# The low-part matmul of an attention score block over 128 array rows instead of 64

## The chip, the cores and the metric

The kernel runs on one core of a Trainium2 chip. The metric is the device time of one launch in microseconds (us), the median of several executions. All work is in 32-bit floats; the matmuls take operands of the type fp32r, and the kernel keeps the accuracy by splitting an operand into a high and a low part and adding up the products.

## What is computed

Two layers of a decoder block on 512 tokens of width 1024. Each layer projects the normalised tokens once; the columns go to a state-space mixer (SSD), a stick-breaking attention of four heads and a block-sparse softmax attention with ALiBi (MoBA) of four heads, all heads 64 wide. Then come an output projection and a SwiGLU FFN.

```
def hybrid_layer(x, ...):
    h = rms_norm(x, pre_mix_norm)
    proj = h @ w_in
    z, xbc, dt_raw, sb_qkv, moba_qkv = jnp.split(proj, [o1, o2, o3, o4], axis=-1)
    y_ssd = ssd_mixer(z, xbc, dt_raw, ...)
    ...
    y_sb = _merge_heads(stick_breaking_attention(q, k, v))
    ...
    y_moba = _merge_heads(moba_attention(q, k, v, alibi_slopes(MOBA_HEADS)))
    ...
    mix = jnp.concatenate([y_ssd, y_sb, y_moba], axis=-1) @ w_out
    x = x + rms_norm(mix, post_mix_norm)
    h2 = rms_norm(x, pre_ffn_norm)
    f = (jax.nn.silu(h2 @ w_gate) * (h2 @ w_up)) @ w_down
    return x + rms_norm(f, post_ffn_norm)

def stick_breaking_attention(q, k, v):
    ...
        z = jnp.einsum('bhqd,bhkd->bhqk', q[:, :, start:end], k[:, :, :end]) * scale
        ...
        log_keep = jnp.where(strict, jax.nn.log_sigmoid(-z), 0.0)
        after = lax.cumsum(log_keep, axis=3, reverse=True) - log_keep
        w = jnp.where(strict, jnp.exp(jax.nn.log_sigmoid(z) + after), 0.0)
```

The change touches the score products of both attentions: `z` here, and the logits of MoBA, which are a product of the same kind over the 64 columns of a head.

## The kernel before

**Staging.** Everything of a layer stays on the chip: 128-partition tiles of 512 columns, named `F0` to `F44`, `R0` to `R7` and `x00` to `x31` (the residual stream), and eight PSUM banks `B0` to `B7`. The weights stream in chunks of 512 KB (`chunk`): SyncE issues the load into `wr`, ScalarE makes the high part `wh` (L108), VectorE the low part `wl` (L109). A projection (`fm_mm`, matmul at L210; `tok_proj`, L201) makes three passes for each of eight 128-row slices of the contraction.

**The score products.** `qk_pair` makes, for two heads, five tiles. `tiles[2 + h]` is the stationary operand of head h: the high part in the head's own 64 partitions (`own`, 0 to 63 for h = 0, 64 to 127 for h = 1) and the low part in the other 64. `tiles[h]` is the moving operand with the high part in both halves, so that one matmul over 128 rows (L300) gives high times high plus low times high. `tiles[4]` holds the low parts of the moving operand of both heads, each in its own 64 partitions. The second matmul (L301) adds high times low: it runs over the head's 64 rows alone, `tiles[2 + h][rows, cs]` against `tiles[4][rows, cd]`.

**Loops.** In stick-breaking attention (`sb_head`, heads 0 to 3), key block i of 3, 2, 1, 0 makes a score block of 128, 256, 384 and 512 columns: the pair L300 and L301, a mask matmul (L315, bf16), then softplus on VectorE and ScalarE (L220, L143, L223), the split of its result (L108, L109), the cumulative sum as matmuls (L322), exp, and the product with v (L329). In MoBA, query block j of 0 to 3 and head h make the pair with 128 to 512 columns, then L425, exp, transposes (L431) and the product with v (L435). So there are 4 heads times 4 blocks in each attention, 32 pairs in a layer and 64 in all, 16 of each width.

**Order.** A scheduler fixes each engine's order when the kernel is built. It mixes the matmuls of the attentions with those of projections that are ready (L210: q and k of the next heads, x, B and C of the SSD; the dt projection L349, and L356, which adds up its parts with 16 rows), so that TensorE has work while VectorE and ScalarE make the softplus.

**GpSimd** has little to do: the power -1/2 of the norms (L155, 50 instructions of one to four columns), and from its queue the DMAs of the decay rows (L379, L387).

**Tiles that are shared.** The twenty q/k tiles of a layer take the places `F4` to `F11` and `x00` to `x31` (`QNAMES`) in groups of five. The last pair of MoBA takes the first group's tiles again. Afterwards the places serve other things: `load_x` fetches the residual again (L99), and `F4` to `F11` hold z and the mixer's output. `XBC`, the SSD's inputs, is `F12` to `F19`.

Of the kernel before, what the change touches and what calls it, by code (L numbers as in the profile page):

```python
# [8 lines left out]
F32 = mybir.dt.float32  # L9
# [7 lines left out]
P = 128  # L17
D = 1024
S = 512
NT = S // P  # L20
# [37 lines left out]
def trunk(ctx, tc, x, wch, wdt, gains, mixgain, conv, small, ident_d, consts_d, stack_d, out):  # L58
# [6 lines left out]

    F = [None if 4 <= i < 12 else cp.tile([P, 512], F32, name=f"F{i}") for i in range(NF)]
    R = [cp.tile([P, 512], F32R, name=f"R{i}") for i in range(8)]
# [90 lines left out]
    def to_fm(srcs, dst, bank):  # L158
        """Token-major [128, 128] slices to feature-major hi and lo parts; dst(i, n) names n consecutive targets."""
        for q in range(0, len(srcs), 4):  # L160
            n = min(4, len(srcs) - q)
            p = bank()
            for i in range(n):
                T.transpose(p[:, i * P:(i + 1) * P], srcs[q + i], ident)  # L164
            dst(q, n, p)
# [27 lines left out]
    def tok_proj(l, c0, bank, evict, w=None):  # L193
        """512 columns, token-major: chunks c0..c0+3 each hold two k tiles."""
        w = w or [chunk(l, c0 + i) for i in range(4)]
        for t in range(NT):
            p = bank()
            n = 0
            for k in range(KT):
                for a, b in PASSES:  # L200
                    T.matmul(p, hT[a][:, k, t * P:(t + 1) * P], w[k // 2][b][:, (k % 2) * 512:(k % 2 + 1) * 512],  # L201
                             start=n == 0, stop=n == 3 * KT - 1)
                    n += 1
            evict(t, p)
# [19 lines left out]

    VT, XBC, LM = F[0:4], F[12:20], F[20:28]
    MIXA, MG = F[28:32], F[32:34]
    QNAMES = [f"F{i}" for i in range(4, 12)] + [f"x{t}{h}" for t in range(NT) for h in range(2)]
    take_jk = ring([F[0:2], F[2:4], F[43:45]])
# [31 lines left out]
    for l in range(DEPTH):  # L260
        # ---- input projection: v, q and k of both attentions, dt
        tok_proj(l, C_V, ring([B[0], B[2], B[4], B[6]]), lambda t, p: A.activation(VT[t], p, AF.Copy),
# [16 lines left out]
        def qk_pair(dup, stk, scale_dup, scale_stk, tiles):  # L279
            """Two heads: [hi; lo] of the stationary operand and [hi; hi] of the moving one, with the latter's lo."""  # L280
            low = tiles[4]
            p = fm_proj(l, dup, acc())
            with tc.high_priority(offset=EV_OFF):
                for h in range(2):
                    own, other, d = slice(h * 64, h * 64 + 64), slice(64 - h * 64, 128 - h * 64), tiles[h]
                    A.activation(d[own], p[own], AF.Copy, scale=scale_dup)
                    V.scalar_tensor_tensor(low[own], p[own], scale_dup, d.bitcast(F32)[own], op0=OP.mult, op1=OP.subtract)
                    A.activation(d[other], p[own], AF.Copy, scale=scale_dup)  # L288
# [9 lines left out]
        def qk_mm(p, tiles, h, cs, cd, stop):  # L298
            rows = slice(h * 64, h * 64 + 64)
            T.matmul(p, tiles[2 + h][:, cs], tiles[h][:, cd], start=True, stop=False, skip_group_check=True)  # L300
            T.matmul(p, tiles[2 + h][rows, cs], tiles[4][rows, cd], start=False, stop=stop, skip_group_check=True)  # L301

        # ---- stick-breaking attention, a head at a time
        sb_mx = ring(B[6:8])
# [29 lines left out]

        SB = [qk_pair(C_SQK, C_SQK + 2, 0.125, 1.0, QS[0:5])]
        exp_set()
        for h in (0, 1):
            if Q1POS == h + 1:
                SB.append(qk_pair(C_SQK + 1, C_SQK + 3, 0.125, 1.0, QS[5:10]))
            sb_head(h)  # L340
        if Q1POS == 0:
            SB.append(qk_pair(C_SQK + 1, C_SQK + 3, 0.125, 1.0, QS[5:10]))

# [50 lines left out]

        MB = [qk_pair(C_MQK + 2, C_MQK, 1.0, qs[:, 0:1], QS[10:15])]
        for h in (2, 3):
            if MBPOS == h - 1:
                MB.append(qk_pair(C_MQK + 3, C_MQK + 1, 1.0, qs[:, 1:2], QS[0:5]))
            sb_head(h)
        if MBPOS == 3:  # L400
            MB.append(qk_pair(C_MQK + 3, C_MQK + 1, 1.0, qs[:, 1:2], QS[0:5]))

# [8 lines left out]

        # ---- softmax attention with ALiBi
        mx = ring([B[3], B[4]])
# [34 lines left out]
        QF = [slot(f"F{i}") for i in range(4, 12)]  # L448
        ZS, MIX = QF[0:4], QF[4:8]
        xres[:] = [[slot(f"x{t}{h}") for h in range(2)] for t in range(NT)]  # L450
        for t in range(NT):
            load_x(t, x if l == 0 else xsave)

        # ---- x, B, C: projection, causal convolution, silu; z
        for i in range(8):
# [9 lines left out]

        # ---- SSD, chunk by chunk
        mx = ring(B[3:5])
# [68 lines left out]

        # ---- output projection, two token tiles at a time
        grow1 = load_row(gains[l, 1], F[41:43])
# [33 lines left out]

        # ---- FFN
        GT = F[12:20] + F[22:28] + QF
        take_p = ring([B[5:7], [B[7], B[0]], [B[2], B[4]], [B[1], B[3]]])
# [98 lines left out]
```

## Time and profile before

| what | value |
|---|---|
| median of 3 runs | 1283.4 us (1283.39 to 1283.61) |
| span of the profiled execution, first to last instruction | 1279.0 us |
| TensorE (PE) busy | 1254.5 us, 98% |
| TensorE weight loads (PEld) busy, beside the matmuls | 1040.3 us, 81% |
| VectorE (DVE) busy | 613.8 us, 48% |
| ScalarE (ACT) busy | 499.0 us, 39% |
| GpSimd (POOL) busy | 45.6 us, 4% |
| granted TensorE clock, mean | 0.999 of full speed |
| DMA | 128.70 MB, mean 101 GB/s |

The median lies 4.4 us above the span: what a launch takes outside the first and the last instruction. "Busy" of TensorE does not mean that the array works at its best: the ends of matmuls are modelled, and a matmul that stands behind something slow is shown as longer, not as a gap. So what a matmul costs in a row of them is read from the starts: the time from one start to the next, called a step here. A row of a timeline gives the start, the duration, the engine, the source line, what is written and read, the shape (rows*columns of the stationary operand, then rows x columns of the moving one) and how many instructions the row joins.

### The profile page before, as it was taken

To read this page: it belongs to the slowest core of one execution; us is meant where nothing else is said; L and a number is where in the kernel's file an instruction comes from. 1 tells how busy PE (TensorE), PEld (TensorE's weight loads), DVE (VectorE), ACT (ScalarE), POOL (GpSimd) and SP (SyncE) were. 2 spreads that over 40 slices of the span, in tenths; PEclk is the share of its full clock that TensorE was granted. 3 is DMA by queue.
4 is the path that set the end of the run, shared out by engine and by line. 5 is a ranking of instruction groups with operands and counts; after the bars stand their busy time and mean duration, and the time that the engine had idled before them with its cause. 6 is when DMAs were issued, how large, how long until landed. Compare 5 with 4: busy or idle time off the path is not lost.

```text
span 1279.0 us, 15353 instructions
## 1 busy us (share of the span) xinstructions
PE 1254.5 (98%) x6118; PEld 1040.3 (81%) x6118; DVE 613.8 (48%) x1011; ACT 499.0 (39%) x892; POOL 45.6 (4%) x72
## 2 busy tenths in 40 slices
PE   6999999999999999999999999999999999999997
PEld 5777788888888888888877788888988888888886
DVE  5456765884322222333465577478642222223334
ACT  5555655353222222322355556634432222222222
POOL 0010000010000000000000100001000000000000
PEclk9999999999999999999999999999999999999999
DMA  7331133333233332332333322222433333332321
GB/s 246 116 102 65 65 108 107 108 132 94 91 98 97 99 99 99 99 96 91 110 114 109 117 66 66 83 91 83 132 116 99 99 99 99 95 93 95 98 83 66
DMA packets 40760, 128.70 MB, mean 101 GB/s; under 512 B 5456, under 2 KB 5744, under 8 KB 40688
## 3 DMA queue, kind: packets, MB, share of 16 engines
q1 hardware_dynamic: 39344, 123.49, 30.3%
q0 software_dynamic: 1344, 4.23, 1.0%
q8 instruction: 48, 0.79, 0.3%
q14 instruction: 24, 0.20, 0.0%
HBM read 123.47 MB, written 4.23 MB: 100 GB/s over the span
## 4 chain that ended last, share of the span: by engine, by line
PE 95%; DVE 2%; ACT 1%; issue 1%; DMA 0%; SPq 0%; DVEq 0%; POOLq 0%; POOL 0%
PE B L210 51%; PE B L596 18%; PE B L201 7%; PE B L546 7%; PE B L301 2%; PE B L322 2%; PE B L329 1%; PE B L435 1%; PE B L300 1%; PE B L164 1%; PE B L506 1%; PE B L431 1%; PE B L349 1%; PE B L557 0%; PE B L512 0%
## 5 line engine op out<-in xcount | busy, mean ns | idle before, releaser
L210 PE MATMUL B<-hT,wh 128*128 128x512 f32 (+1 forms) x2048 | 609.1, 379 | 2.2 <-ACT F L288 2.2
L210 PEld LDWEIGHTS B<-hT,wh 128*128 128x128 f32 x2048 | 374.7, 188 | 73.4 <-ACT F L288 3.3
L210 PE MATMUL B<-hT,wl 128*128 128x512 f32 (+1 forms) x1024 | 386.6, 378 | 0.0
L109 DVE TENSOR_TENSOR wl<-wr,wh 128x1024 fp32r<-128x1024 f32 x204 | 248.6, 1224 | 254.7 <-ACT wh L108 253.2
L108 ACT ACTIVATE wh<-wr 128x1024 fp32r<-128x1024 f32 x204 | 214.9, 1057 | 392.8 <-PE B L210 314.5
L210 PEld LDWEIGHTS B<-hT,wl 128*128 128x128 f32 x1024 | 192.8, 188 | 34.5 <-issue 0.4
L596 PE MATMUL B<-wh,R 128*128 128x512 f32 x704 | 190.1, 389 | 0.0
L596 PEld LDWEIGHTS B<-wh,R 128*128 128x128 f32 x704 | 132.1, 188 | 27.3
L596 PE MATMUL B<-wl,R 128*128 128x512 f32 x352 | 110.0, 389 | 0.0
L109 DVE TENSOR_TENSOR R<-F,R 128x512 fp32r<-128x512 f32 (+2 forms) x76 | 45.9, 607 | 122.2 <-ACT R L108 121.9
L108 ACT ACTIVATE R<-F 128x512 fp32r<-128x512 f32 (+2 forms) x76 | 42.4, 560 | 143.6 <-PE B L596 139.0
L587 DVE TENSOR_TENSOR F<-B,F 128x512 f32<-128x512 f32 x44 | 30.4, 691 | 127.3 <-PE B L210 127.3
L201 PE MATMUL B<-wh,hT 128*128 128x512 f32 x256 | 83.2, 400 | 2.4 <-DVE hT L109 2.4
L596 PEld LDWEIGHTS B<-wl,R 128*128 128x128 f32 x352 | 66.1, 188 | 13.8
L546 PE MATMUL B<-wh,R 128*128 128x512 f32 x256 | 76.9, 398 | 0.0
L155 POOL TENSOR_TENSOR SM<-SM,mhalf 128x1 f32<-128x1 f32 (+2 forms) x50 | 35.5, 712 | 1097.7 <-DVE SM L154 793.7
L201 PEld LDWEIGHTS B<-wh,hT 128*128 128x128 f32 x256 | 48.1, 191 | 13.3 <-DVE hT L109 2.8
L546 PEld LDWEIGHTS B<-wh,R 128*128 128x128 f32 x256 | 47.6, 188 | 9.9 <-DVE R L109 0.4
L201 PE MATMUL B<-wl,hT 128*128 128x512 f32 x128 | 50.6, 396 | 0.0
L143 ACT ACTIVATE F<-F 128x512 f32<-128x512 f32 (+3 forms) x80 | 39.1, 498 | 21.0 <-DVE F L220 20.4
L546 PE MATMUL B<-wl,R 128*128 128x512 f32 x128 | 43.0, 394 | 0.0
L461 DVE SCALAR_TENSOR_TENSOR F<-B,cw,F 128x511 f32<-128x511 f32 (+2 forms) x48 | 35.8, 745 | 11.8 <-ACT F L459 11.2
(145 smaller groups left out, 988.2 us busy)
## 6 DMA issues: line engine op xcount, KB each, us to landing
wr<-in_wch_dram SPq DMA_DIRECT2D x204, 512.0 KB, 3.6
x<-in_x_dram SPq DMA_DIRECT2D x16, 256.0 KB, 3.2
F<-in_gains_dram SPq DMA_DIRECT2D x16, 256.0 KB, 4.3
F<-acd POOLq DMA_DIRECT2D x16, 256.0 KB, 6.4
xsave<-x SPq DMA_DIRECT2D x8, 256.0 KB, 2.0
x<-xsave SPq DMA_DIRECT2D x8, 256.0 KB, 2.9
out_dram<-x SPq DMA_DIRECT2D x8, 256.0 KB, 2.0
F<-in_mixgain_dram SPq DMA_DIRECT2D x4, 256.0 KB, 4.9
```

The costliest lines, as they stand in the source:

```text
L108: A.activation(hi, src, AF.Copy)
L109: return eng.tensor_tensor(lo, src, hi.bitcast(F32), op=OP.subtract)
L143: order["exp"][group] = A.activation(o, i, f, **kw)
L155: G.tensor_tensor(r, m, mhalf[:, 0:n], op=OP.pow)
L201: T.matmul(p, hT[a][:, k, t * P:(t + 1) * P], w[k // 2][b][:, (k % 2) * 512:(k % 2 + 1) * 512], start=n == 0, stop=n == 3 * KT - 1)
L210: T.matmul(p[:, t0 * P:t1 * P], w[b][:, k * P:(k + 1) * P], hT[a][:, k, t0 * P:t1 * P], start=first and n == 0, stop=n == 3 * KT - 1, skip ...
L301: T.matmul(p, tiles[2 + h][rows, cs], tiles[4][rows, cd], start=False, stop=stop, skip_group_check=True)
L322: T.matmul(pz[:, o:w], ntri if i2 == i else nones, s2, start=False, stop=i2 == NT - 1 and n == 1, skip_group_check=True)
L461: V.scalar_tensor_tensor(u[:, j:], p[:, :S - j], cw[:, i, 3 - j:4 - j], u[:, j:], op0=OP.mult, op1=OP.add)
L546: T.matmul(OB[j][hf], lt, w[b][:, hf * 512:(hf + 1) * 512], start=k == ks[0] and a == 0 and b == 0, stop=k == ks[-1] and a == 1)
L587: V.tensor_tensor(GT[i], pu, sg, op=OP.mult)
L596: T.matmul(B[2 * t + hf], gs[a][:, t * P:(t + 1) * P], w[b][:, hf * 512:(hf + 1) * 512], start=i == 0 and a == 0 and b == 0, stop=i == HT ...
```

## The change

`qk_pair` now makes six tiles: each head has a low tile of its own, `tiles[4 + h]`. GpSimd first fills the 64 partitions of the other head in it with zeros, VectorE writes the low part into the head's own 64 as before. The second matmul takes all 128 rows: the stationary operand is the same slice `tiles[2 + h][:, cs]` as the first one's, and the zeros keep the other half out of the sum. The twenty q/k tiles become 24 in groups of six; `F18` and `F19` join their places, and the last two tiles of `XBC` are taken there later.

```diff
-    F = [None if 4 <= i < 12 else cp.tile([P, 512], F32, name=f"F{i}") for i in range(NF)]
+    F = [None if 4 <= i < 12 or 18 <= i < 20 else cp.tile([P, 512], F32, name=f"F{i}") for i in range(NF)]
...
-    VT, XBC, LM = F[0:4], F[12:20], F[20:28]
+    VT, LM = F[0:4], F[20:28]
...
-    QNAMES = [f"F{i}" for i in range(4, 12)] + [f"x{t}{h}" for t in range(NT) for h in range(2)]
+    QNAMES = [f"F{i}" for i in range(4, 12)] + [f"x{t}{h}" for t in range(NT) for h in range(2)] + ["F18", "F19"]
...
         def qk_pair(dup, stk, scale_dup, scale_stk, tiles):
-            low = tiles[4]
+            for h in range(2):
+                G.memset(tiles[4 + h].bitcast(F32)[64 - h * 64:128 - h * 64], 0.0)
             p = fm_proj(l, dup, acc())
...
                     own, other, d = slice(h * 64, h * 64 + 64), slice(64 - h * 64, 128 - h * 64), tiles[h]
+                    low = tiles[4 + h]
...
         def qk_mm(p, tiles, h, cs, cd, stop):
-            rows = slice(h * 64, h * 64 + 64)
             T.matmul(p, tiles[2 + h][:, cs], tiles[h][:, cd], start=True, stop=False, skip_group_check=True)
-            T.matmul(p, tiles[2 + h][rows, cs], tiles[4][rows, cd], start=False, stop=stop, skip_group_check=True)
+            T.matmul(p, tiles[2 + h][:, cs], tiles[4 + h][:, cd], start=False, stop=stop, skip_group_check=True)
...
-        SB = [qk_pair(C_SQK, C_SQK + 2, 0.125, 1.0, QS[0:5])]
+        SB = [qk_pair(C_SQK, C_SQK + 2, 0.125, 1.0, QS[0:6])]
...
-            SB.append(qk_pair(C_SQK + 1, C_SQK + 3, 0.125, 1.0, QS[5:10]))
+            SB.append(qk_pair(C_SQK + 1, C_SQK + 3, 0.125, 1.0, QS[6:12]))
...
-        MB = [qk_pair(C_MQK + 2, C_MQK, 1.0, qs[:, 0:1], QS[10:15])]
+        MB = [qk_pair(C_MQK + 2, C_MQK, 1.0, qs[:, 0:1], QS[12:18])]
...
-            MB.append(qk_pair(C_MQK + 3, C_MQK + 1, 1.0, qs[:, 1:2], QS[0:5]))
+            MB.append(qk_pair(C_MQK + 3, C_MQK + 1, 1.0, qs[:, 1:2], QS[0:6]))
...
+        XBC = F[12:18] + [slot("F18"), slot("F19")]
```

In the built program, TensorE, VectorE and ScalarE hold the same instructions in the same order as before, with other tiles in some places. Two queues are different: GpSimd gets 16 fills of 64x512, and SyncE's reloads of the residual stand elsewhere.

GpSimd (POOL), from the norms of the first layer's mixer to the decay DMA of the second layer. `SM` holds small columns, `mhalf` the exponent; `F18`, `F19`, `F8`, `F9`, `x10`, `x11` are the low tiles of the second layer. Before:

```order
L155 TENSOR_TENSOR SM_129<-SM_129,mhalf_147 128x1 x3
L155 TENSOR_TENSOR SM_129<-SM_129,mhalf_147 128x4
L155 TENSOR_TENSOR SM_129<-SM_129,mhalf_147 128x1
L155 TENSOR_TENSOR SM_129<-SM_129,mhalf_147 128x2 x4
L155 TENSOR_TENSOR SM_129<-SM_129,mhalf_147 128x1 x16
L379 DMA acd1_4680<-acT_4678 32x128
```

Now, from the eight powers of the first layer's output projection on:

```order
L155 TENSOR_TENSOR SM_127<-SM_127,mhalf_145 128x1 x8
L283 MEMSET F18_4379 64x512
L283 MEMSET F19_4380 64x512
L283 MEMSET F8_4367 64x512
L283 MEMSET F9_4368 64x512
L155 TENSOR_TENSOR SM_127<-SM_127,mhalf_145 128x1 x4
L283 MEMSET x10_4373 64x512
L283 MEMSET x11_4374 64x512
L155 TENSOR_TENSOR SM_127<-SM_127,mhalf_145 128x1 x4
L283 MEMSET F8_4367 64x512
L381 DMA acd1_4696<-acT_4694 32x128
```

The sixteen powers of the output projection and of the layer boundary were one run; now four fills stand before the eight of the boundary and two (on `x10` and `x11`) between its fourth and its fifth. In the first layer the same fills stand at the head of the queue (four ahead of the first power) and between the second and the third power (two).

SyncE (SP), the loads of weights (`wr`) and the reload of the residual in the first layer. Before:

```order
L122 DMA wr2_120<-in_wch_dram 128x1024
L99 DMA x00_1237<-in_x_dram 128x512
L99 DMA x01_1238<-in_x_dram 128x512
L122 DMA wr0_118<-in_wch_dram 128x1024
L99 DMA x10_1239<-in_x_dram 128x512
L99 DMA x20_1241<-in_x_dram 128x512
L99 DMA x11_1240<-in_x_dram 128x512
L99 DMA x21_1242<-in_x_dram 128x512
L99 DMA x30_1243<-in_x_dram 128x512
L122 DMA wr1_119<-in_wch_dram 128x1024
```

Now:

```order
L99 DMA x00_1247<-in_x_dram 128x512
L99 DMA x10_1249<-in_x_dram 128x512
L122 DMA wr0_116<-in_wch_dram 128x1024
L122 DMA wr1_117<-in_wch_dram 128x1024
L122 DMA wr2_118<-in_wch_dram 128x1024
L99 DMA x01_1248<-in_x_dram 128x512
L99 DMA x11_1250<-in_x_dram 128x512
L122 DMA wr0_116<-in_wch_dram 128x1024
L99 DMA x20_1251<-in_x_dram 128x512
L99 DMA x30_1253<-in_x_dram 128x512
L99 DMA x21_1252<-in_x_dram 128x512
L99 DMA x31_1254<-in_x_dram 128x512
```

Two reloads (`x00`, `x10`) moved ahead of three weight loads; `x31`, which stood far ahead of the others in the queue since no pair used its place, now stands last.

## Rows read from the trace of the kernel before

**Rows 1.** Page, part 4: the chain that ended last, by engine.

```profile
PE 95%; DVE 2%; ACT 1%; issue 1%; DMA 0%; SPq 0%; DVEq 0%; POOLq 0%; POOL 0%
```

**Rows 2.** Busy time by stretch: stretch, us; PE, PEld, DVE, ACT, POOL; clock, DMA.

```profile
55.50:190.00 134.50, 133.16 (x689) 105.61 (x688) 87.46 (x218) 79.62 (x176) 7.70 (x13) 1.00 0.26 84
```

**Rows 3.** Timeline of PE, 55 to 57 us: start, duration, engine, line, operation.

```profile
55.51 0.22 PE L300 MATMUL B<-F,F 128*128 128x128 f32 x1
...
55.96 0.36 PE L300 MATMUL B<-F,F 128*128 128x256 f32 x1
56.25 0.38 PE L301 MATMUL B<-F,F 64*128 64x256 f32 x1
56.56 0.23 PE L315 MATMUL B<-smaskb,identb 128*128 128x128 bf16 x1
56.60 0.48 PE L210 MATMUL B<-hT,wh 128*128 128x512 f32 x1
56.92 0.40 PE L210 MATMUL B<-hT,wl 128*128 128x512 f32 x1
57.15 0.63 PE L210 MATMUL B<-hT,wh 128*128 128x512 f32 x2
```

**Rows 4.** Timeline of the weight loads (PEld) in the same stretch.

```profile
56.25 0.18 PEld L301 LDWEIGHTS B<-F,F 64*128 64x128 f32 x1
```

**Rows 5.** Timeline of PE elsewhere: 128-row matmuls behind 128-row ones.

```profile
62.64 0.33 PE L322 MATMUL B<-R,nones 128*128 128x128 f32 x2
62.81 0.40 PE L349 MATMUL B<-hT,wd 128*16 128x512 f32 x1
...
92.06 0.28 PE L322 MATMUL B<-R,ntri 128*128 128x256 f32 x1
92.17 0.22 PE L300 MATMUL B<-x,x 128*128 128x128 f32 x1
```

**Rows 6.** Timeline of PE around another change of the row count (L356, 16 rows).

```profile
72.59 1.05 PE L356 MATMUL B<-stack,F 16*128 16x8 f32 x8
73.57 0.50 PE L210 MATMUL B<-hT,wl 128*128 128x512 f32 x1
73.91 0.62 PE L210 MATMUL B<-hT,wh 128*128 128x512 f32 x2
```

**Rows 7.** Timeline of PE at the last of the 64 pairs (two L201 between).

```profile
819.47 0.48 PE L300 MATMUL B<-F,F 128*128 128x512 f32 x1
...
820.87 0.40 PE L201 MATMUL B<-wl,hT 128*128 128x512 f32 x1
```

**Rows 8.** Timeline of PE before the waits at 103 us; brackets: idle before.

```profile
100.82 0.30 PE L300 MATMUL B<-x,x 128*128 128x128 f32 x1
...
102.97 0.43 PE L435 MATMUL B<-F,F 128*128 128x64 f32 x2 [0.64 <-ACT F L433]
```

**Rows 9.** Timeline of ACT at the same place.

```profile
100.99 1.06 ACT L108 ACTIVATE wh<-wr 128x1024 fp32r<-128x1024 f32 x1 [0.52 <-PE B L210]
```

**Rows 10.** Timelines of DVE and PE at the wait with the least cover.

```profile
61.10 0.63 DVE L109 TENSOR_TENSOR R<-F,R 128x128 fp32r<-128x128 f32 x2
...
62.18 0.62 PE L322 MATMUL B<-R,ntri 128*128 128x128 f32 x4
```

**Rows 11.** Timeline of POOL: the first power, and the fifth of the layer boundary.

```profile
5.21 0.55 POOL L155 TENSOR_TENSOR SM<-SM,mhalf 128x1 f32<-128x1 f32 x1 [4.76 <-DVE SM L154]
...
647.11 0.55 POOL L155 TENSOR_TENSOR SM<-SM,mhalf 128x1 f32<-128x1 f32 x1 [7.86 <-DVE SM L154]
```

**Rows 12.** Timeline of DVE at the same two places.

```profile
6.94 1.42 DVE L179 SCALAR_TENSOR_TENSOR F<-x,SM,F 128x512 f32<-128x512 f32 x2 [1.81 <-DMA F<-in_gains_dram]
...
639.29 1.42 DVE L179 SCALAR_TENSOR_TENSOR F<-x,SM,F 128x512 f32<-128x512 f32 x2 [0.66 <-POOL SM L155]
```

**Rows 13.** Groups by line and shape: busy us, mean ns | idle before, releaser.

```profile
L288 ACT ACTIVATE F<-B 64x512 fp32r<-64x512 f32 x12 | 7.1, 593 | 6.0 <-DVE F L287 4.3 <-DVE x L287 1.4
```

More of the change, by code (lines that the diff above doesn't have):

```diff
@@ L338, in trunk @@
             if Q1POS == h + 1:
-                SB.append(qk_pair(C_SQK + 1, C_SQK + 3, 0.125, 1.0, QS[5:10]))
+                SB.append(qk_pair(C_SQK + 1, C_SQK + 3, 0.125, 1.0, QS[6:12]))
             sb_head(h)
         if Q1POS == 0:
-            SB.append(qk_pair(C_SQK + 1, C_SQK + 3, 0.125, 1.0, QS[5:10]))
+            SB.append(qk_pair(C_SQK + 1, C_SQK + 3, 0.125, 1.0, QS[6:12]))
         pd = acc()
@@ L393, in decay @@
             expf(LM[i], LM[i], group="L")
-        MB = [qk_pair(C_MQK + 2, C_MQK, 1.0, qs[:, 0:1], QS[10:15])]
+        MB = [qk_pair(C_MQK + 2, C_MQK, 1.0, qs[:, 0:1], QS[12:18])]
         for h in (2, 3):
             if MBPOS == h - 1:
-                MB.append(qk_pair(C_MQK + 3, C_MQK + 1, 1.0, qs[:, 1:2], QS[0:5]))
+                MB.append(qk_pair(C_MQK + 3, C_MQK + 1, 1.0, qs[:, 1:2], QS[0:6]))
             sb_head(h)
         if MBPOS == 3:
-            MB.append(qk_pair(C_MQK + 3, C_MQK + 1, 1.0, qs[:, 1:2], QS[0:5]))
+            MB.append(qk_pair(C_MQK + 3, C_MQK + 1, 1.0, qs[:, 1:2], QS[0:6]))
         ss = sm(4)
@@ L571, in trunk @@
                     pre_norm(j, grow2, take_jk(), ring(OB[j] if j < 2 else OB[j][0:1]))
-        GT = F[12:20] + F[22:28] + QF
+        GT = XBC + F[22:28] + QF
         take_p = ring([B[5:7], [B[7], B[0]], [B[2], B[4]], [B[1], B[3]]])
```

## The prediction

> **What bounds the kernel now.** I read the chain that ended last first: TensorE (PE) holds 95% of it [rows 1]. Then the stretch in which the change lies: from 55.5 to 190 us PE is busy 133.2 of 134.5 us at full clock, VectorE (DVE) 87.5, ScalarE (ACT) 79.6 [rows 2]; the other layer's stretch reads alike. So a microsecond that PE saves there is a microsecond of the kernel, unless PE then meets work that is not ready. Since the page counts a matmul that stands behind something slow as a long one, "busy" hides what the change is about, and I went to the starts. In a plain row, a 512-column matmul follows the last one after 0.23 us (56.92 to 57.15) [rows 3], a 256-column one after 0.12, two of 128 columns after 0.17 together, 0.085 each [rows 5]; 384 lies half-way between 256 and 512, 0.175. I call these the plain steps.
>
> Around the 64-row matmul the steps are longer. At 55.96 the first matmul (L300) of 256 columns starts; L301 follows after 0.29, the mask matmul after another 0.31 [rows 3]. The weights of L301 begin to load at 56.25, together with the matmul's own record [rows 4]: they were not fetched under L300. The same comes behind L301, where the rows go back from 64 to 128: the L210 at 56.60 is followed only after 0.32 instead of 0.23. That this belongs to the change of the row count, not to the score products, is seen at the small matmuls of the dt projection (L356), which have 16 rows, other tiles and another bank: behind them the first L210 takes 0.34 until the next one, again with a weight load of its own in it [rows 6]. Matmuls of 128 rows that add into one bank (the L322) show nothing of it [rows 5].
>
> **What the pairs give back.** For each pair I take the time from the start of L300 to the start of the second instruction behind the pair (behind the mask matmul in the stick-breaking heads), so that the late weight load is inside, and take the plain steps of the same instructions off. The mask matmul has no plain neighbour in the trace; it goes in at 0.06, between its own step of 0.04 [rows 3] and the 0.085 of other 128-column ones. At 55.96: 56.92 - 55.96 = 0.96, less 0.12 + 0.12 + 0.06 + 0.23 = 0.53, leaves 0.43. The first pair, at 55.51: from there to 56.25 are 0.74, less 0.085 + 0.085 + 0.06 + 0.12 = 0.35, leaves 0.39. The last, a MoBA pair of 512 columns: 820.87 - 819.47 = 1.40, less four steps of 0.23, leaves 0.48 [rows 7]. Done for all 64, from the first of these to the last, the losses lie between 0.31 and 0.49 with a mean of 0.42, about half of it on either side of L301: **26.8 us**. With 128 rows no row count changes within a pair, and both matmuls even use the same stationary slice, so I take all of it as gone.
>
> The bounds of that sum: with 0.06 for every 128-column step and 0.04 for the mask matmul 28.2 us; with 0.11 (the longer of the two steps within those 0.17) and 0.085 for the mask 25.2 us.
>
> **What PE then waits for.** PE runs in a fixed order that the change leaves as it is. For each wait of PE in both stretches I compared the end of the work that it waits for with PE's start, and followed that work back to the matmul which released it: only pairs between release and use shorten the cover. Most waits keep 2 to 5 us. The one with the least cover is that of the four L322 from 62.18 on, of which the last two take a low part that DVE ends at 61.73, 0.45 us before the first [rows 10]; no pair lies between its release and its use, so both move together. One place in each layer has no cover: at 102.97 PE already stands for 0.64 us [rows 8], behind a run of ACT that a matmul released just before 100.99 [rows 9]. The pair at 100.82 lies between, its 0.37 us turn into a longer wait: twice 0.37 = **0.75 us lost**. Everything later (SSD, output projection, FFN) is released by matmuls behind the last pair and moves along.
>
> **What is added.** Sixteen fills of 64x512 on GpSimd (POOL). The trace has no such fill; the nearest row by shape is ACT's copy of 64x512, 0.59 us, the nearest on POOL the power, 0.55 us for one column [rows 11] and 1.02 for four [rows 13]. I take 0.6, since a fill has no arithmetic; from below 0; the slope of the powers, 0.16 a column, would make it some 80 us and is kept for a rival. What hides them: the four at the head of the queue are in front of the first power at 5.21, whose result DVE uses only at 6.94, when the gains have landed [rows 11, 12]: some 5.7 us for four, free up to 1.4 us each. At the layer boundary `x10` and `x11` may be filled when DVE has read them (639.29 + 1.42 = 640.71) and the store of them has landed, and the next power comes at 647.11 [rows 11, 12]: some 6 us for two, free up to 3 us each. In the first layer, between the second and the third power, the room is like that. The four before the boundary stand in a queue that has nothing to do. The fills of `F8` and `F9` for the last pair of tiles end many microseconds ahead of the L301 that waits for them. Cost: 0; and 4 us for each microsecond beyond 1.4 at the start, 2 at each of the two other places. A fill that shares the SBUF with DVE may slow it at the boundary, where PE waits for DVE; I keep up to 2 us for it in the range.
>
> SyncE's two reloads ahead of three weight loads wait for the last pair of head 2, which ends before the next weight buffer comes free; the others wait for the same pairs as before. Cost 0.
>
> **The sum.** 26.8 - 0.75 = 26.05 us. The profiled execution would have a span of 1279.0 - 26.05 = 1252.95; the median stands 4.4 us above the span, and the forecast is 1283.4 - 26.05 = 1257.35, say **1257.3 us**. Its own range: 28.2 - 0.75 = 27.45 us of gain at best, 1255.95, and with as much again as the second decimals of the rows leave open 1255; 25.2 - 0.75 = 24.45 at least, 1258.95, and with 2 us for the fills at the boundary and some 3 us for covers of DVE and ACT that shrink (their busy share in the stretch goes from 65 and 59% to 72 and 66%, since it gets 10% shorter) 1264.
>
> **Rivals.** First: only half is gained, because the weights of the second matmul still can't be loaded under the first. The lost 0.42 of a pair are two changes of some 0.2, and each holds a bare weight load of 0.11: the 0.34 of the first L210 behind the 16-row matmuls less the plain 0.23 [rows 3, 6]. If those loads stay bare and only the rest goes, the gain is 64 x (0.42 - 2 x 0.11) = 12.8 us: 1270.6. Against it: L210 loads 128 rows for each of its matmuls and steps by 0.23 all the same, and two L322 of 128 columns by 0.085, less than a bare load alone would take [rows 3, 5]. The Trainium skill ("TensorE: Matmul & The Clock Gate", Part 3, "The mechanism") speaks for this rival: it says that a weight load overlaps a matmul in flight only when the two have different row groups, and two matmuls over all rows never do. By that rule alone each full-row matmul of this kernel would stand behind a bare load; the trace disagrees. Chance 6%.
>
> Second: nothing is gained, since the delay belongs to something that stays (two heads' tiles, the bank of the scores): 1283.4. Against it are the 16-row matmuls, which show it elsewhere, and the L322. That the change does not do what it says is excluded by the diff: both operands lose their row slice. Chance 4%.
>
> Third, slower: the fills. If POOL needs t us for one, the start costs 4 (t - 1.4) and the two places behind it 2 (t - 3) each; 8 t - 17.6 exceeds the 26.05 us from t = 5.5 on. At 8 us it would be 1257.35 + 46.4 = 1303.75. For it: POOL's power grows by 0.16 us a column, so a slow engine is not excluded. Against it: a fill computes nothing, and ACT copies the same shape in 0.59 us [rows 13]. Chance 5%.
>
> **How the numbers follow.** Forecast 85%, rivals 6, 4 and 5%. The range is that of the forecast, 1255 to 1264, and leaves out the rivals and a small part beside. A measurement of this kernel can tell some 0.2% from no change, 2.6 us: faster 91%, same 4%, slower 5%.
>
> **What would show it.** Right: L303 (the second matmul's new line) steps behind L302 by 0.085 to 0.23 us by its width, its weight load starts ahead of it, and the L210 behind a pair has no 0.32 step; the stretch 55.5 to 190 is 13 us shorter; the wait near 100 us grows by 0.3 to 0.4. Wrong, for the first rival: L303 still starts with its load. For the third: the first power comes later than 6.4 us or the fifth power of the boundary stands behind a fill. New waits of PE for DVE or ACT inside the stretch would show that the covers were overrated.

## The result

The changed kernel took 1264.9 us (median of four runs, 1262.4 to 1266.2) against 1283.5: the ratio is 0.9857, 95% interval 0.9841 to 0.9873. The forecast was 1257.3 with a range of 1255 to 1264. The direction was right, the size was not: 18.6 us came, not 26.05, and the time lies 0.9 us above the range. The profiled execution has a span of 1260.6 us against 1279.0.

How these numbers hang together can only be read with the granted clock: of 41 runs of the kernel before beside the experiments, 17 took 1280.6 to 1281.9 us at a mean clock of 0.999 and 24 took 1283.0 to 1284.6 at 0.996 or 0.997, and of eight runs of the changed kernel three took 1260.9 to 1262.4 at 0.998, one 1263.6 at 0.996 and four 1266.1 to 1266.7 at 0.994 or 0.995. So part of what separates two runs of one kernel is TensorE's clock, and the worth of the rows is best read between executions in which it does not fall: 1279.0 us for before and 1259.1 for the changed kernel run again (e1_again), **19.9 us**.

### The profile page after: what moved, and what is told of

Read it like the earlier page. It is cut to its first block, busy times and chain, and to the rows that moved or that the text cites. A ratio compares the mean times of both kernels' runs of the same rounds, so it can differ in the third digit from the quotient of the medians.

```text
span 1260.6 us, 15385 instructions
## 1 busy us (share of the span) xinstructions
PE 1235.3 (98%) x6118; PEld 1037.5 (82%) x6118; DVE 612.5 (49%) x1011; ACT 498.6 (40%) x892; POOL 53.8 (4%) x88
## 4 chain that ended last, share of the span: by engine, by line
PE 95%; DVE 2%; ACT 1%; issue 1%; DMA 0%; SPq 0%; DVEq 0%; POOLq 0%; POOL 0%; ACTq 0%
PE B L210 52%; PE B L599 18%; PE B L201 7%; PE B L549 7%; PE B L324 2%; PE B L331 1%; PE B L437 1%; PE B L302 1%; PE B L164 1%; PE B L509 1%; PE B L303 1%; PE B L433 1%; PE B L351 1%; PE B L560 0%; PE B L515 0%
## 5 line engine op out<-in xcount | busy, mean ns | idle before, releaser
L210 PE MATMUL B<-hT,wh 128*128 128x512 f32 (+1 forms) x2048 | 609.0, 379 | 2.2 <-ACT F L291 2.2
L210 PEld LDWEIGHTS B<-hT,wh 128*128 128x128 f32 x2048 | 376.1, 189 | 71.6 <-ACT F L291 3.3
L210 PE MATMUL B<-hT,wl 128*128 128x512 f32 (+1 forms) x1024 | 386.6, 378 | 0.0
L210 PEld LDWEIGHTS B<-hT,wl 128*128 128x128 f32 x1024 | 193.3, 189 | 33.7
L201 PE MATMUL B<-wh,hT 128*128 128x512 f32 x256 | 82.7, 399 | 2.4 <-DVE hT L109 2.4
L201 PEld LDWEIGHTS B<-wh,hT 128*128 128x128 f32 x256 | 48.0, 190 | 12.9 <-DVE hT L109 2.9
L201 PE MATMUL B<-wl,hT 128*128 128x512 f32 x128 | 50.5, 394 | 0.0
```

Of the source, the lines that this page charges most:

```text
L210: T.matmul(p[:, t0 * P:t1 * P], w[b][:, k * P:(k + 1) * P], hT[a][:, k, t0 * P:t1 * P], start=first and n == 0, stop=n == 3 * KT - 1, skip ...
```

## The profile after

The chain that ended last (page, part 4, by engine) is as before, [rows 1]: PE holds it.

```profile
PE 95%; DVE 2%; ACT 1%; issue 1%; DMA 0%; SPq 0%; DVEq 0%; POOLq 0%; POOL 0%; ACTq 0%
```

Busy time by stretch (us of the stretch; PE, PEld, DVE, ACT, POOL, each with its instructions; granted clock, DMA share, GB/s) from just before the first pair of the first layer to the last one, of before:

```profile
55.50:189.36 133.86, 132.52 (x687) 105.13 (x685) 86.82 (x217) 79.47 (x176) 7.70 (x13) 1.00 0.26 83
```

and of after:

```profile
55.30:179.50 124.20, 122.56 (x687) 103.37 (x687) 85.92 (x216) 79.07 (x176) 8.74 (x15) 1.00 0.29 91
```

The same 687 matmuls stand in it, and the stretch is 9.66 us shorter at full clock, not 13. PE stays 99% busy: nothing new stands in its way, the steps gave back less than I had summed.

The place of [rows 3] in the timeline of PE after (start, duration, engine, line, operation):

```profile
55.12 0.39 PE L210 MATMUL B<-hT,wh 128*128 128x512 f32 x1
55.35 0.22 PE L302 MATMUL B<-F,F 128*128 128x128 f32 x1
55.41 0.28 PE L303 MATMUL B<-F,F 128*128 128x128 f32 x1
55.53 0.23 PE L317 MATMUL B<-smaskb,identb 128*128 128x128 bf16 x1
55.57 0.36 PE L302 MATMUL B<-F,F 128*128 128x256 f32 x1
55.77 0.28 PE L303 MATMUL B<-F,F 128*128 128x256 f32 x1
55.89 0.23 PE L317 MATMUL B<-smaskb,identb 128*128 128x128 bf16 x1
55.93 0.48 PE L210 MATMUL B<-hT,wh 128*128 128x512 f32 x1
56.24 0.40 PE L210 MATMUL B<-hT,wl 128*128 128x512 f32 x1
```

L303 is followed by the mask after 0.12 where it was 0.31, and stands 0.20 behind a 256-column L302 where L301 stood 0.29. But the L210 behind the mask still takes 0.31 until the next one (55.93 to 56.24), as the one at 56.60 did, with 0.32 [rows 3]. I had put that step down to the rows.

The wait near 100 us grew as foreseen, from 0.64 [rows 8] to 0.93 us, and the one behind it stayed:

```profile
100.35 0.43 PE L437 MATMUL B<-F,F 128*128 128x64 f32 x2 [0.93 <-ACT F L435]
101.49 0.50 PE L210 MATMUL B<-hT,wh 128*128 128x512 f32 x1 [0.70 <-ACT F L291]
```

The fills are cheap. On POOL the four at the start end at 2.97, and the first power waits 2.56 us more for its input, which comes from DVE:

```profile
0.73 2.24 POOL L283 MEMSET F<- 64x512 f32 x4 [0.29 <-POOLq L667]
5.53 0.55 POOL L155 TENSOR_TENSOR SM<-SM,mhalf 128x1 f32<-128x1 f32 x1 [2.56 <-DVE SM L154]
```

One thing is new. The place of this wait in the second layer, near 721 us, of after (columns as above):

```profile
718.85:722.25 3.40, 1.97 (x13) 1.55 (x12) 3.27 (x7) 3.12 (x6) 0.43 (x1) 1.00 0.01 2
722.26:725.67 3.41, 3.23 (x8) 2.55 (x9) 2.18 (x4) 2.84 (x7) 0.00 (x0) 0.50 0.50 154
```

and of the same kernel run again:

```profile
718.85:722.25 3.40, 1.96 (x13) 1.55 (x12) 3.27 (x7) 3.12 (x6) 0.43 (x1) 1.00 0.01 2
722.26:725.67 3.41, 3.23 (x14) 2.68 (x15) 2.18 (x4) 2.83 (x7) 0.00 (x0) 1.00 0.49 154
```

PE did the same ahead of 722.26: it stood for 0.92 us, ran a little and began to stand for 0.70. Then in one execution the clock is granted at half (1.2 instead of 2.4 GHz) for 3.41 us, in which 8 matmuls lie instead of 14, and in the other it stays full.

## The experiments

In the kernels that add a line, the lines behind it count one or two higher than in the kernel that they alter.

**e1_again: the changed kernel, unchanged.** On one chip with the three that follow.

> The changed kernel once more, for its spread and for the granted clock of each run. Theory A (the pairs give back 20.3 us, and the lengthened wait of PE near 100 us and near 721 us now and then lets the clock fall for some 3.4 us, at a price of about 1.4 us each time): the runs lie between 1261 and 1267 us, and those with a lower mean clock are the longer ones; where the profile shows a stretch at half clock, it begins within the wait near 100 or 721 us or just behind it. Rival B (the spread has another cause, such as DMA): times and clock are not in step, or the fall stands elsewhere.

Measured: 1263.7 us (1260.9, 1261.4, 1266.1, 1266.7), ratio 0.9855 (0.9834 to 0.9876). The profiled execution, 1260.9 us with a span of 1259.1, has no fall of the clock until its last microseconds and gives the 19.9 us above.

**e2_sb_only and e3_moba_only: one half of the pairs each.** In e2 the MoBA pairs keep 64 rows (they are the ones that set `stop`):

```
-            T.matmul(p, tiles[2 + h][:, cs], tiles[4 + h][:, cd], start=False, stop=stop, skip_group_check=True)
+            rows = slice(h * 64, h * 64 + 64) if stop else slice(0, P)
+            T.matmul(p, tiles[2 + h][rows, cs], tiles[4 + h][rows, cd], start=False, stop=stop, skip_group_check=True)
```

and in e3 the two slices change places.

> Only the 32 pairs of the stick-breaking heads run over 128 rows; the MoBA pairs take the head's 64 rows again, the fills and the order stay. Theory A: the pairs of the stick-breaking heads give back some 9 us, so 1274.5; the pair that lies between the release and the wait near 101 us is a MoBA pair, so this wait stays at 0.64 us as before the change, the clock does not fall there and the runs lie within 1 us. Rival B (fills or zeros disturb the clock): the runs scatter by several us all the same. Rival C (the gain belongs to something that only all pairs together change): well above 1278.

> Only the 32 MoBA pairs run over 128 rows. Theory A: they give back some 11 us, less 0.6 for the wait near 100 us, which grows to 0.93 as in the changed kernel: 1273 us where the clock does not fall, and up to 4 us more where it does, median about 1274.5; gain of this and of the stick-breaking pairs alone add up to that of the change within 2 us. Rival B: the wait stays at 0.64, or the runs do not scatter.

Measured: 1275.9 us, ratio 0.9941 (0.9927 to 0.9955), and 1271.6, 0.9919 (0.9905 to 0.9934). Against 1283.2 that is 7.3 and 11.6 us, together 18.8, where both at once give 19.5. The gains add up within the spread of the runs, and the masked half gives less; e3 came 2.9 us below its expected median. On the clock e2 speaks against a simple story: its waits of PE have the length they had before (0.64 and 0.70), and yet the clock fell behind them in both layers, at 102.73 and at 730.78. A longer wait is not what a fall takes. Nor does it bring one each time: e3 has the longer wait in both layers (0.94 and 0.92) and one fall, at 731.24.

**e4_ones: ones in the place of the zeros** (so that a wrong term is added to the scores).

```
-                G.memset(tiles[4 + h].bitcast(F32)[64 - h * 64:128 - h * 64], 0.0)
+                G.memset(tiles[4 + h].bitcast(F32)[64 - h * 64:128 - h * 64], 1.0)
```

> The changed kernel with ones instead of zeros in the other head's rows (which adds a wrong term to the scores; nothing is left out). Theory A: time and spread as of the changed kernel, 1261 to 1267 us, since the data have no part in it. Rival B (zeros in half of the rows let the clock fall): no fall, all runs within 1 us, at 1261.

Measured: 1266.0 us (1265.7 to 1266.8), ratio 0.9873 (0.986 to 0.9887), within the changed kernel's own runs. The profile has three falls of 3.41 us and a span of 1264.0: 4.9 us above that without one, some 1.6 for each. Zeros are not the cause of the falls.

**e5_rows32: 32 rows instead of 64**, in the kernel before.

```
-            T.matmul(p, tiles[2 + h][rows, cs], tiles[4][rows, cd], start=False, stop=stop, skip_group_check=True)
+            rows32 = slice(h * 64, h * 64 + 32)
+            T.matmul(p, tiles[2 + h][rows32, cs], tiles[4][rows32, cd], start=False, stop=stop, skip_group_check=True)
```

> The kernel before with the second matmul of each pair over the first 32 of the head's 64 rows, so that half of the low part of the moving operand is left out. The order of all engines is that of the kernel before. Theory (a change of the row count costs some 0.2 us whatever the counts are, and one before and one behind the second matmul make the 0.42 us of a pair): L301 still steps 0.29 behind a 256-column L300 and the pair still loses 0.42, so the time is that of the kernel before, 1283.2 us, within 1.5 us. Rival (the cost grows with the rows that are left out or added, 96 instead of 64): each pair loses 0.63, and 64 x 0.21 = 13.4 us are added: 1296.6. Rival (what was lost is work of the missing or present rows themselves): half the rows, some 6 us in either direction.

Measured: 1281.4 us, ratio 0.9993 (0.9982 to 1.0004). The timeline of PE:

```profile
58.05 0.36 PE L300 MATMUL B<-F,F 128*128 128x256 f32 x1
58.34 0.38 PE L302 MATMUL B<-F,F 32*128 32x256 f32 x1
58.66 0.23 PE L316 MATMUL B<-smaskb,identb 128*128 128x128 bf16 x1
```

0.29 and 0.32, where 64 rows gave 0.29 and 0.31 [rows 3]. (This execution stood some 2 us later from its start on, ahead of any pair.) What costs is that the count changes; 32 or 64 rows make no difference.

**e6_both64: the first matmul over 64 rows too**, in the kernel before (the product of one low part is left out).

```
-            T.matmul(p, tiles[2 + h][:, cs], tiles[h][:, cd], start=True, stop=False, skip_group_check=True)
+            T.matmul(p, tiles[2 + h][rows, cs], tiles[h][rows, cd], start=True, stop=False, skip_group_check=True)
```

> The kernel before with the first matmul of each pair too over the head's 64 rows, so that the product of the low part of one operand with the other is left out (some matmuls and copies stand at other places in the order for it, since the 64 rows need less of their operands). Theory (changes of the row count cost, wherever they stand): the change moves from between the two matmuls to ahead of the first; the second follows the first by a plain step of 0.085 to 0.23 us with its weights loaded ahead, but the first stands 0.2 us late behind its neighbour of 128 rows, and there are still two changes a pair: 1283 us, within 3 us. Rival (what costs is the second matmul as such, which adds into the bank of the first from another slice of the same tile): the pair's inner step stays 0.29 for 256 columns, and the ends get a change more, 64 x 0.2 = 12.8 us slower or so: 1296. Rival (full rows are the only cure, but half of the loss belongs to the inner step alone): 1270.

Measured: 1280.2 us, ratio 0.9986 (0.9976 to 0.9995). The timeline of PE:

```profile
55.57 0.39 PE L210 MATMUL B<-hT,wh 128*128 128x512 f32 x1
55.89 0.32 PE L300 MATMUL B<-F,F 64*128 64x128 f32 x1
...
56.42 0.38 PE L300 MATMUL B<-F,F 64*128 64x256 f32 x1
56.64 0.28 PE L301 MATMUL B<-F,F 64*128 64x256 f32 x1
56.85 0.23 PE L315 MATMUL B<-smaskb,identb 128*128 128x128 bf16 x1
...
57.20 0.40 PE L210 MATMUL B<-hT,wl 128*128 128x512 f32 x1
```

The delay moved: L300 now stands 0.32 behind a 512-column neighbour, not 0.23, and L301 follows a 256-column L300 after 0.22, close to the 0.20 of the changed kernel. In the kernel before, the L210 ahead of these two pairs starts at

```profile
55.28 0.39 PE L210 MATMUL B<-hT,wh 128*128 128x512 f32 x1
```

From this L210 to the second one behind the pairs are 1.64 us before (to 56.92 [rows 3]), 1.63 in e6 (55.57 to 57.20) and 1.12 in the changed kernel (55.12 to 56.24). The pair is hardly cheaper as long as two changes stand at it. These steps show it better than the time of the whole, since PE's order in e6 is another one from 92 us on.

**e7_wait_gone and e8_wait_gone_before: the wait near 100 us.** A split on ScalarE that is not urgent stands ahead of the copy that PE waits for; here it is made to come later, in the changed kernel and in the one before.

```
-                A.activation(pTs[:, 0:w], pT[:, 0:w], AF.Copy)
+                pt = A.activation(pTs[:, 0:w], pT[:, 0:w], AF.Copy)
+                if j == 0 and h == 0:
+                    order["pt"] = [pt]
...
-            p = fm_proj(l, C_XBC + i, acc())
+            with after(order["pt"] if i == 3 else []):
+                p = fm_proj(l, C_XBC + i, acc())
```

> The changed kernel, and in addition the projection of XBC chunk 3 waits for the copy of the first transposed MoBA block, so that ScalarE's split of its weights no longer stands ahead of that copy; the order of all engines changes behind that place. Theory: the two waits of TensorE near 100 and 721 us (0.93 + 0.70 and 0.92 + 0.70 us) go, which gives 3.2 us against the changed kernel's execution without a clock fall (1260.9), and with them the falls of the clock inside the layers, so that the runs no longer scatter by 5 us: 1257.5 to 1259, all runs within 1.5 us but for other falls. Rival (another wait takes their place, since the chunk is needed later and its split then meets the neighbour's work): 1262 to 1266 as the changed kernel, with a wait of over 0.5 us elsewhere in the stretch. Rival (falls do not belong to these waits): the waits are gone, the median 1260.5, and the runs still scatter by 5 us.

> The same addition in the kernel before (64 rows). Theory: its waits near 103 and 734 us (0.64 + 0.70 each layer) go: 2.7 us less than the kernel before, 1280.5, and against the changed kernel with the same addition the rows are then worth 21 to 23 us, more than the 19.5 that were measured, since no wait takes 0.29 us a layer back and no fall of the clock is added. Rival (the addition makes waits of its own): 1283 or more; the difference between the two kernels with the addition stays 19.5.

Measured: 1263.5 us (1261.9 to 1264.6), ratio 0.9851 (0.9834 to 0.9867), no better than the changed kernel, and 1281.6 us, 0.9988 (0.9978 to 0.9997), between the two forecasts. In e7 the theory fell: the wait of 0.93 is gone, but another of 0.73 stands at L302, and the one behind it is still there with 0.48.

```profile
100.68 0.33 PE L302 MATMUL B<-F,F 128*128 128x128 f32 x1 [0.73 <-DVE F L298]
...
101.61 0.66 PE L210 MATMUL B<-hT,wh 128*128 128x512 f32 x1 [0.48 <-ACT F L291]
```

In e8 they are 0.50 and 0.34. The profile of e7 has falls of the clock at 101.78 and 637.67 all the same. Between the two medians lie 18.0 us, where I expected 21 to 23. Since the waits were exchanged and not removed, the two runs do not show what they cost.

**e9_mask_out and e10_mask_out_before: without the mask matmul**, in the changed kernel and in the one before.

```
-                T.matmul(pz[:, 0:P], identb, smaskb, start=False, stop=False, skip_group_check=True)
```

> The changed kernel without the mask matmul of the 32 stick-breaking pairs (the mask is left out of the scores). Theory (the masked pairs give back less than was summed, because each mask matmul still costs its own 0.04 us and makes the fp32 matmul behind it 0.08 us late with its weights, which the row count does not touch): without it 32 x (0.04 + 0.08) = 3.8 us go, so that the execution without a clock fall comes to 1257 us instead of 1260.9. Rival (the mask costs its plain step of 0.06 and no more): 32 x 0.06 = 1.9 us, 1259.0.

> The kernel before without the mask matmul (the mask is left out of the scores). Theory: there the matmul behind the mask is late for the change of the row count anyway, so only the mask's own step of 0.04 us goes, 32 x 0.04 = 1.3 us: without a clock fall 1279.5 instead of 1280.8. The change is then worth 1279.5 - 1257 = 22.5 us instead of 19.9. Rival (the mask has nothing to do with what was summed too high): both kernels lose the same, and the change stays worth 19.9 us.

Measured: 1272.5 us, ratio 0.9931 (0.9914 to 0.9948), and 1291.2, 1.0072 (1.0053 to 1.009). Both are some 8 to 10 us longer than with the mask, which neither theory has room for. The scheduler reorders the work of all engines behind the first pairs, PE meets waits that it did not have, the clock falls more often (the mean granted clock from 90 to 140 us is 0.86 in both), and so each time alone says nothing on the mask. Their difference says something: PE has one order in both, and the mean clock of both profiled executions is 0.992. The spans, 1287.0 and 1268.6, lie 18.4 us apart, the medians 18.7, nearer to the rival's 19.9 than to the theory's 22.5. Some of PE's waits are longer in e9, so this is no clean price either. The timeline of e9 shows the mask's own price, at a place ahead of all that:

```profile
56.23 0.22 PE L302 MATMUL B<-F,F 128*128 128x128 f32 x1
...
56.40 0.33 PE L302 MATMUL B<-F,F 128*128 128x256 f32 x1
...
56.69 0.39 PE L210 MATMUL B<-hT,wh 128*128 128x512 f32 x1
56.91 0.39 PE L210 MATMUL B<-hT,wl 128*128 128x512 f32 x1
```

From the first L302 to the second L210 are 0.68 us; with two masks it was 56.24 - 55.35 = 0.89. Each mask costs 0.105 instead of the 0.06 that I put in for it, and without it the L210 behind the pair steps by 0.22.

**e11_fills_twice: every fill done twice**, in the changed kernel.

```
                 G.memset(tiles[4 + h].bitcast(F32)[64 - h * 64:128 - h * 64], 0.0)
+                G.memset(tiles[4 + h].bitcast(F32)[64 - h * 64:128 - h * 64], 0.0)
```

> The changed kernel with every one of the sixteen fills done twice. Theory (fills of 0.52 us lie on GpSimd where nobody waits for it): 32 fills instead of 16, the eight at the start end near 5.1 us, before the input of the first power is there, and the time stays that of the changed kernel, 1260.9 to 1266.7 us with its median at 1264 to 1265. Rival (the fills do cost their time at the start and at the layer boundary): 4 x 0.52 + 2 x 2 x 0.52 = 4.2 us more.

Measured: 1266.1 us (1262.2 to 1266.8), ratio 0.987 (0.985 to 0.9889). The median is 1.2 us above that of the changed kernel, inside the spread of its runs, and the profile has three falls of the clock. Eight fills at the start end at 5.27 us and the first power starts at 5.32, where it started at 5.53. No cost is seen.

**e12_dt_rows: the 16-row matmuls of the dt projection over 128 rows**, in the changed kernel.

```
-    stack = cp.tile([16, 8], F32, name="stack")
+    stack = cp.tile([P, 8], F32, name="stack"); nc.vector.memset(stack, 0.0)
...
-        d16 = F[38]
+        d16 = F[38]; G.memset(d16, 0.0)
...
-            T.matmul(pt[:, t * 8:(t + 1) * 8], d16[0:16, t * P:(t + 1) * P], stack, start=t == 0, stop=t == 3,
+            T.matmul(pt[:, t * 8:(t + 1) * 8], d16[:, t * P:(t + 1) * P], stack, start=t == 0, stop=t == 3,
```

> The changed kernel in which the four small matmuls of the dt projection run over all 128 rows too, with zeros in the 112 rows that they did not use, for one more fill in each layer. Theory (any change of the row count costs, wherever it stands): the first 512-column L210 behind them steps by 0.23 instead of 0.34 us, and the matmuls ahead of them no longer stand late; some 0.3 us a layer in the trace, too little for the times: 1260.3 without a clock fall, the median within 1.5 us of the changed kernel. Rival (the cost belongs to the score blocks alone): the step stays 0.34.

Measured: 1265.7 us (1263.9 to 1266.0), ratio 0.987 (0.9855 to 0.9885), no difference that the times can tell. The timeline of PE in the changed kernel:

```profile
70.75 0.61 PE L210 MATMUL B<-hT,wh 128*128 128x512 f32 x2
71.30 1.05 PE L358 MATMUL B<-stack,F 16*128 16x8 f32 x8
72.28 0.50 PE L210 MATMUL B<-hT,wl 128*128 128x512 f32 x1
72.62 0.62 PE L210 MATMUL B<-hT,wh 128*128 128x512 f32 x2
```

and in e12:

```profile
71.54 0.62 PE L210 MATMUL B<-hT,wh 128*128 128x512 f32 x2
72.00 0.95 PE L358 MATMUL B<-stack,F 128*128 128x8 f32 x8
72.81 0.49 PE L210 MATMUL B<-hT,wl 128*128 128x512 f32 x1
73.13 0.63 PE L210 MATMUL B<-hT,wh 128*128 128x512 f32 x2
```

My theory was wrong on the place: with all 128 rows the first L210 still steps by 0.32, not by 0.23. Of the 0.34 that I had read as the price of a row change [rows 6] only 0.02 belong to it. The rest is the price of standing behind a short matmul. What the rows do save there lies ahead: the first small matmul starts 0.46 us behind the start of the two L210 ahead of it, not 0.55, and the eight of them take 0.81 us instead of 0.98. From those two L210 to the second one behind are 1.59 us instead of 1.87. So the two row changes do cost 0.28 us at this place, close to the 0.3 that I had expected and to the price of a pair.

## Why the prediction was right, and where it was wrong

**The mechanism was right.** With 128 rows the second matmul is no longer delayed, and the rows are the cause: the order of the instructions is that of before, e5 shows the same delay for another count, e6 shows it wandering with the place of the change, and e12 shows a like price at the 16-row matmuls of another product. Where a pair stands between long matmuls and has no mask, it costs the plain steps and nothing more. In the timeline of PE before such a pair reads

```profile
127.97 0.28 PE L300 MATMUL B<-x,x 128*128 128x256 f32 x1
128.18 0.38 PE L301 MATMUL B<-x,x 64*128 64x256 f32 x1
128.49 0.73 PE L210 MATMUL B<-hT,wh 128*128 128x512 f32 x2
129.06 0.39 PE L210 MATMUL B<-hT,wl 128*128 128x512 f32 x1
```

and after

```profile
123.55 0.28 PE L302 MATMUL B<-x,x 128*128 128x256 f32 x1
123.67 0.28 PE L303 MATMUL B<-F,x 128*128 128x256 f32 x1
123.78 0.63 PE L210 MATMUL B<-hT,wh 128*128 128x512 f32 x2
124.25 0.40 PE L210 MATMUL B<-hT,wl 128*128 128x512 f32 x1
```

1.09 us became 0.70.

**The step that failed is "so I take all of it as gone".** I measured each pair against plain steps and put the whole difference, 0.42 us, down to the two row changes. Done again for the changed kernel, with the same plain steps, 0.09 us a pair are still there:

| pairs | number | lost before, mean us | lost after, mean us |
|---|---|---|---|
| no mask, right behind a 512-column L210 | 8 | 0.39 | 0.00 |
| no mask, behind short matmuls | 24 | 0.44 | 0.09 |
| mask, right behind a 512-column L210 | 6 | 0.39 | 0.07 |
| mask, behind short matmuls | 26 | 0.41 | 0.12 |

Summed over the 64, 26.8 us before and 5.7 after. The 5.7 never belonged to the rows. They are the price of standing behind a short matmul (the 128-column L324 and L433, the 64-column L331 and L437, the mask). As far as the records tell, such a matmul waits for its own weights. In the changed kernel the weights of the L210 at 55.93 start to load with the mask, and only its 0.04 us lie ahead of that L210:

```profile
55.89 0.20 PEld L210 LDWEIGHTS B<-hT,wh 128*128 128x128 f32 x1
```

No run changed a load by itself, so the weights are argued as the reason; that the price stands behind short matmuls with full rows is shown, by e12 and by the kernel before at a place with 128 rows everywhere:

```profile
126.81 0.33 PE L322 MATMUL B<-R,nones 128*128 128x128 f32 x2
126.98 0.45 PE L210 MATMUL B<-hT,wl 128*128 128x512 f32 x1
127.27 0.62 PE L210 MATMUL B<-hT,wh 128*128 128x512 f32 x2
```

The L210 behind two 128-column matmuls steps by 0.29, not 0.23. I looked at the L322 among themselves and not at what stands behind them, and I took the L210 behind the 16-row matmuls as the proof for the rows, where e12 shows that it was this (what the rows cost there stands ahead of it). The Trainium skill ("TensorE: Matmul & The Clock Gate", "Back-to-back issue gap") says that the spacing in a stream of weight loads and matmuls is set by both; these steps agree.

Another 0.8 us were counted twice, since the windows of pairs that stand next to each other overlap: the one at 55.51 reaches into the one at 55.96. So 26.8 - 5.7 - 0.8 = 20.3 us were to be had, 0.32 a pair. My lower bound of 25.2 varied the second decimal of the plain steps, and not the question whether the neighbours of a pair are plain.

**The waits.** The one at 100 us grew by 0.29 us, and its twin in the other layer by 0.28 (forecast 0.37 each). No other appeared. 20.3 - 0.6 = 19.7, and the two executions without a fall stand 19.9 apart: the account closes within 0.2 us. That DVE and ACT have covers enough was right, and so was the cost of the fills: 0.52 us each against an estimate of 0.6, and nothing for the time; at the layer boundary the two of `x10` and `x11` are done at 631.71 and the next power comes at 637.16. The moved reloads on SyncE cost nothing that a wait of PE shows. The 3 us of the range for shrinking covers and 2 for the fills were not used; without them the time would have been further outside. A fill of 512 columns is as short as a power of one column; the slope of the powers, 0.16 us a column, on which the third rival rested, would have made it some 80 us.

**The clock was not foreseen**, in two ways. First, the level: I noted that the median stood 4.4 us above the profiled span and added it as a constant. Around the span lie 1.8 us; the other 2.6 are the lower mean clock of those runs, which the profiled one did not have. Second, the changed kernel has more of it: up to three falls in an execution (the profiles of e4, e11 and e12 have three), each some 1.6 us. In the median of before the clock takes 2.6 us, in that of the changed kernel 4.0 (1264.9 - 1.8 - 1259.1). That makes the step from 1263.5 (1283.4 - 19.9) to the measured 1264.9, and with it the range missed; but 1263.5 too lies inside the range only by the 5 us kept for covers and fills, which were not needed. Which execution falls, and why the changed kernel does so more often, stays open. e2 speaks against the length of the waits, e4 against the zeros, e7 did not get rid of the waits, and a kernel with no wait at that place in the same order was not found.

**The rivals.** That the weights of the second matmul stay bare is refuted: in the changed kernel's timeline of the weight loads

```profile
123.55 0.19 PEld L303 LDWEIGHTS B<-F,x 128*128 128x128 f32 x1
```

L303 starts to load with L302's matmul and begins 0.12 us later at its plain place. The Trainium skill ("TensorE: Matmul & The Clock Gate", Part 3, "The mechanism") says in its list that a load overlaps a matmul in flight only when the row groups differ. This load disagrees, since both matmuls run over all rows, and the measurement decides; the same section also names a background weight buffer as a second case, which would allow it. But a weaker form of that rival seems to hold: behind a short matmul the load is only partly covered, with full rows too, and by the records this is the 5.7 us. That nothing is gained, and that the fills cost the gain, are refuted by the result and by e11.

## What to carry to other kernels

A matmul over fewer rows than its neighbours is not cheaper: in this kernel each of the 64 score matmuls cost 0.32 us for its two changes of the row count, and zeros in the missing rows gave that back for a fill that nobody waits for. Before a step that looks late is put down to one cause, look for the same neighbours without that cause in the same trace: the matmul behind a short one is late anyway. And compare a profiled span only with runs of the same mean clock; what stands between span and median is not a constant.

## What the runs showed of the hardware

- A change of the row count cost the same for 32 rows as for 64: the steps are 0.29 and 0.32 with 32 rows (e5), 0.29 and 0.31 with 64. At the 16-row matmuls the two changes cost 0.28 us (e12), in a score pair 0.32.
- A 512-column matmul steps by 0.23 us behind its like, 0.29 behind two of 128 columns and 0.31 to 0.32 behind a mask of one short step (0.04) or eight of 8 columns, all at full rows and full clock.
- Behind the same work of PE (a wait of 0.92 us, a few matmuls, a wait of 0.70) the clock once fell to half for 3.41 us and once stayed full.
- A fill of 64x512 on GpSimd takes 0.52 us, about as long as a power of one column there (0.55).
